# Softmax scaling and duplicate key rows moved from VectorE to ScalarE in a two-layer hybrid trunk

## The chip, the cores and the metric

The kernel runs on one core of a Trainium2 chip. A core has TensorE (matrix products, PE in the profile, with its weight loads as PEld), VectorE (DVE), ScalarE (ACT), GpSimd (POOL) and SyncE (SP), which here issues the transfers from HBM. Each engine carries out its own instructions in order and waits on semaphores for the results of the others. The metric is the device time of one execution in microseconds (us), lower is better.

## The reference

The reference is a trunk of two layers over 512 latent tokens `x` and 256 context tokens `y`, model width 1024. In each layer a normalised, modulated input is projected by `w_in`; three branches run on the parts of the projection; their gated outputs are merged and projected back.

```python
def hybrid_layer(x, y, ...):
    rq, rk, rv, rg, nq, nk, nv, ng, gq, gk, gv, gg, mg = split_cols(hx @ w_in)      # latent
    crq, ..., cgv, cgg, cmg = split_cols(hy @ w_in)                                   # context
    o_lat, o_ctx = bidir_retention(...)                    # 4 heads of 128
    na_x = neighbourhood_attention(nq, nk, nv, kc, vc, rpb, rows) * silu(ng)  # 8 heads of 64
    gqa_x = gqa_blocks(q_g, k_all, v_all) * silu(gg)        # 8 query heads, 2 key/value heads of 64
    x = x + gate_x * merge_branches(ret_x, na_x, gqa_x, mg, w_ret_o, w_na_o, w_gqa_o, w_out)
    if need_ctx:  # layer 0 only
        y = y + gate_y * merge_branches(ret_y, na_y, gqa_y, cmg, ...)

def attend(q, k, v):                      # grouped-query attention; the context's attention too
    s = einsum('btkgd,bskd->bkgts', q, k) * dh ** -0.5
    return einsum('bkgts,bskd->btkgd', softmax(s), v)

# neighbourhood attention: a query sees a window of 8 rows x 16 columns of the grid, and the context
s = where(col_ok, einsum(q, k_window) * scale + bias, -inf)
p = softmax(concatenate([s, einsum(q, k_ctx) * scale]))
```

The result is `rms_norm(x, final_norm_w)`. What matters here are the two softmaxes, neighbourhood attention (NA below) and grouped-query attention (GQA), and the keys of NA.

## The kernel before

Every product is made in split precision. A value is kept as a rounded high part and a low part (the rest), and `mm3` (L285 to L288) makes one product of three matmuls: high by high, high by low, low by high. So each operand has to be split before TensorE can use it: a ScalarE copy writes the high part, a subtraction writes the low part. For the streamed weights that is `whi` on ScalarE (L270) and `wlo` on GpSimd (L272).

The order of TensorE's instructions is written out by hand; the other engines are ordered by a scheduler that follows the order in which the code issues them, with priorities in a few places. In the code, `window()` takes two lists: the steps of a branch (scores, transposes, products with the values) and `Unit`s (projections and merges, which are long rows of matmuls on streamed weights). After each step it lets units run until their share of the work is done, so that between two dependent steps of a softmax there is independent TensorE work. The windows of the two softmax branches are `na.steps(p)` and `gqa.steps(p)`, with p from 0 to 3 in each of two layers. In the profiled execution NA of layer 0 lies at about 50 to 260 us, GQA of layer 0 at 290 to 525, NA of layer 1 at 1010 to 1160, GQA of layer 1 at 1160 to 1380. PSUM banks are few: `pj` 2, `s` 2, `pt` 3, `pv` 1.

The path of one block of probabilities, in NA's `s_step` and in GQA's:

1. TensorE makes the scores in an `s` bank (L603 in NA; L859, L860 in GQA).
2. VectorE takes them to SBUF and finds the row maximum (L606 with the bias added; L861), then makes its negative, `nm` (L613; L866, L868).
3. ScalarE takes the exponential of two tiles with `nm` as the bias and the row sum as accumulated output (L615, 128x512; L870, 128x768).
4. VectorE makes the reciprocals `rc` of both sums in one instruction (L617; L872).
5. The two tiles are scaled by `rc`: the one on VectorE, the other on GpSimd (L620; L875).
6. TensorE transposes 128x128 pieces into a `pt` bank (L632; L883).
7. `split_pt` splits the bank: ScalarE copies the high part `ph` (L446), VectorE subtracts for the low part `pl` (L447).
8. TensorE multiplies the values with `ph`, then with `pl` (L643, L644; L895).

In layer 0 each NA head has a small softmax over the context besides, `ctx_steps`: two exponentials on ScalarE (`pc`, L465), reciprocals on VectorE (`rcc`, L467), two scalings on GpSimd (L469), transposes (L477), the split, the products (L485).

The keys of NA come from the projection unit `u_k(p)`, one pair of heads at a time, in two column blocks (512 and 256). From the PSUM bank `ps`, `split_rows` (L432 to L436) writes the high parts of 64 rows on ScalarE (L434) and the low parts on VectorE (L435), for each of the two heads. The score matmul takes 128 rows: the high keys twice, one above the other. So the 64 high rows are written a second time into the other 64 partitions of the same tile, by L544 and L545.

Of the kernel before, what the change touches and what calls it, by code (L numbers as in the profile page):

```python
# [12 lines left out]
AF = mybir.ActivationFunctionType  # L13
ALU = mybir.AluOpType
# [25 lines left out]
def trunk_kernel(ctx: ExitStack, tc: tile.TileContext, xt, wcol, wv, adaw, wbr, wout, nabias, vecs,  # L40
                 cst, cst16, out, taps=None):
    nc = tc.nc
# [19 lines left out]
    def f(ap):  # L62
        return ap.bitcast(F32)
# [368 lines left out]
    def split_rows(hi, lo, rl, r0, src, scale, cols):  # L432
        rows = slice(r0, r0 + 64)
        nc.scalar.activation(hi[rows, cols], src[rows], AF.Copy, scale=scale)  # L434
        nc.vector.scalar_tensor_tensor(lo[rl:rl + 64, cols], src[rows], scale, f(hi[rows, cols]),  # L435
                                       op0=ALU.mult, op1=ALU.subtract)  # L436
# [58 lines left out]
    def pv_(P, j):  # L495
        t, pad = P[j]
        return t[:, :, pad:pad + 256]


    class NA:  # L500
# [34 lines left out]
        def u_k(self, p):  # L535
            def ev(ps, o, n):
                if o == 0:
                    self.K1[p] = [self.ap.tile([128, NT], F32R, tag="k1", name="k1", bufs=4) for _ in range(2)]
                    self.K2[p] = self.kz[p % 2]
                c = slice(o, o + n)  # L540
                K1, K2 = self.K1[p], self.K2[p]
                split_rows(K1[0], K2[0], 0, 0, ps, 1.0, c)
                split_rows(K1[1], K2[1], 64, 64, ps, 1.0, c)
                nc.vector.tensor_copy(K1[0][64:128, c], f(K1[0][0:64, c]))  # L544
                nc.vector.tensor_copy(K1[1][0:64, c], f(K1[1][64:128, c]))  # L545
            return u_proj(ap_wcol[self.l][CT_NK + p], G_ALL, ev)

        def u_v(self, p):
# [26 lines left out]
        def heads(self, p):  # L575

            ap, l = self.wp, self.l
            heads = []
            for e in range(2):
                r0 = 64 * e  # L580
                st = {}

                def start(e=e, st=st):
                    bias = ap.tile([128, 4, 256], F32, tag="bias", name="bias", bufs=2)
                    nc.sync.dma_start(out=bias[:, 0:3, :], in_=nabias[l, 2 * p + e].rearrange("p (v c) -> p v c", c=256))
                    nc.gpsimd.memset(bias[:, 3, :], 0.0)
                    pa = ap.tile([128, 2, 2, 256], F32, tag="pa", name="pa", bufs=2)
                    pb = ap.tile([128, 2, 2, 320], F32, tag="pb", name="pb", bufs=2)
                    nc.gpsimd.memset(pb[:, :, :, 0:64], 0.0)
                    P = [(pa[:, 0], 0), (pb[:, 0], 64), (pb[:, 1], 64), (pa[:, 1], 0)]  # L590
                    st.update(bias=bias, P=P)
                    for nm in ("mx", "nm", "sm", "rc"):
                        st[nm] = ap.tile([128, 4], F32, tag=nm, name=nm, bufs=2)

                def s_step(j, e=e, st=st, start=start):
                    Q, K1, K2 = self.Q[p], self.K1[p], self.K2[p]
                    if j == 0:
                        start()
                    P, bias = st["P"], st["bias"]
                    s = bank("s")  # L600
                    qc = slice(128 * j, 128 * j + 128)
                    kc = 64 * BAND0[j]
                    mm(s, lhsT=Q[e][:, qc], rhs=two_blocks(K1[e], kc, NX, 256), start=True, stop=False)  # L603
                    mm(s, lhsT=Q[e][:, qc], rhs=two_blocks(K2[e], kc, NX, 256), start=False, stop=True)
                    v = BVAR[j]
                    nc.vector.tensor_tensor_reduce(  # L606
                        out=pv_(P, j), in0=s.rearrange("p (a c) -> p a c", a=2),
                        in1=bias[:, v:4:3 - v, :], scale=1.0, scalar=-3.0e38, op0=ALU.add, op1=ALU.max,
                        accum_out=st["mx"][:, j:j + 1])
                    if j % 2 == 0:  # L610
                        return
                    h = slice(j - 1, j + 1)
                    nc.vector.tensor_scalar(st["nm"][:, h], st["mx"][:, h], -1.0, None, op0=ALU.mult)  # L613
                    for i in (j - 1, j):
                        nc.scalar.activation(pv_(P, i), pv_(P, i), AF.Exp,  # L615
                                             bias=st["nm"][:, i:i + 1], accum_out=st["sm"][:, i:i + 1])
                    nc.vector.reciprocal(st["rc"][:, h], st["sm"][:, h])  # L617
                    for i in (j - 1, j):
                        eng = nc.gpsimd if i % 2 else nc.vector
                        eng.tensor_scalar(pv_(P, i), pv_(P, i), st["rc"][:, i:i + 1], 1.0, op0=ALU.mult, op1=ALU.mult)  # L620

                jobs = [(4 + c, 0, [(j, (256, 384, 384, 256)[j] + 128 * c) for j in range(4)]) for c in range(2)]
                for t in (0, 1, 2, 3):
                    js = [j for j in range(4) if abs(j - t) <= 1]
                    jobs.append((t, js[0], [(j, 64 * (2 * t - BAND0[j]) + (0, 64, 64, 0)[j]) for j in js]))

                def t_step(i, st=st, jobs=jobs):
                    tb, q0, parts = jobs[i]
                    pt = bank("pt")
                    for a, (j, c) in enumerate(parts):  # L630
                        pj = st["P"][j][0].rearrange("p a c -> p (a c)")
                        nc.tensor.transpose(pt[:, a * 128:a * 128 + 128], pj[:, c:c + 128], ident)  # L632
                    st[i] = split_pt(pt, 128 * len(parts), ap, 3)

                def pv_step(i, e=e, st=st, jobs=jobs, r0=r0):
                    tb, q0, parts = jobs[i]
                    n = 128 * len(parts)
                    if i == 0:
                        st["ops"] = bank("pv")
                    ph, pl = st[i]  # L640
                    V = self.V[p]
                    o = st["ops"][:, 128 * q0:128 * q0 + n]
                    mm(o, lhsT=V[:, tb, e, :], rhs=ph[:, :n], start=(i == 0), stop=False)  # L643
                    mm(o, lhsT=V[:, tb, e, :], rhs=pl[:, :n], start=False, stop=(i == len(jobs) - 1))  # L644
                    if i == len(jobs) - 1:
                        pv_out(st["ops"], NX, self.get_ot(p), r0, 0)

                def smm(s, e=e):
                    Q, K1, K2 = self.Q[p], self.K1[p], self.K2[p]
                    for i in range(2):  # L650
                        qc = slice(NX + 128 * i, NX + 128 * i + 128)
                        o = s[:, 256 * i:256 * i + 256]
                        mm(o, lhsT=Q[e][:, qc], rhs=K1[e][:, NX:NT], start=True, stop=False)
                        mm(o, lhsT=Q[e][:, qc], rhs=K2[e][:, NX:NT], start=False, stop=True)
                S = [(0.7, 0.45, lambda j=j, s_step=s_step: s_step(j)) for j in range(4)]
                T = [(1.0, 0.4, lambda i=i, t_step=t_step: t_step(i)) for i in range(6)]
                PV = [(1.0, 0.4, lambda i=i, pv_step=pv_step: pv_step(i)) for i in range(6)]
                X = [] if l else list(ctx_steps(st, smm, lambda: None, lambda e=e: [self.V[p][:, 4 + c, e, :] for c in range(2)],
                                                lambda: self.get_ot(p), r0, ap, 3))
                heads.append((S, T, PV, X))  # L660
            return heads
# [28 lines left out]
    class GQA:  # L690
# [145 lines left out]
        def steps(self, p):  # L836
            ap, l = self.ap, self.l
            kv = p // 2
            Q, K1, K2, V = self.Q, self.K1[kv], self.K2[kv], self.V
# [3 lines left out]
            for e in range(2):  # L843
                for hf in range(2):
                    st = {}

                    def s_step(i, e=e, hf=hf, st=st):
                        jj, u = divmod(i, 2)
                        if i == 0:
                            st["P"] = ap.tile([128, 2, NT], F32, tag="p", name="p", bufs=2)  # L850
                            st["mx"] = ap.tile([128, 4], F32, tag="mx", name="mx", bufs=2)
                            for nm in ("nm", "sm", "rc"):
                                st[nm] = ap.tile([128, 2], F32, tag=nm, name=nm, bufs=2)
                        P, mx, nm, sm, rc = (st[x] for x in ("P", "mx", "nm", "sm", "rc"))
                        j = 2 * hf + jj
# [6 lines left out]
                                                op1=ALU.max, accum_out=mx[:, i:i + 1])  # L862
# [6 lines left out]
                        for a in range(2):  # L869
                            nc.scalar.activation(P[:, a], P[:, a], AF.Exp, bias=nm[:, a:a + 1],  # L870
                                                 scale=rqe[:, 2 * hf + a:2 * hf + a + 1], accum_out=sm[:, a:a + 1])
                        nc.vector.reciprocal(rc, sm)  # L872
                        for a in range(2):
                            eng = nc.gpsimd if a else nc.vector
                            eng.tensor_scalar(P[:, a], P[:, a], rc[:, a:a + 1], 1.0, op0=ALU.mult, op1=ALU.mult)  # L875

                    def t_step(t2, st=st):
                        pt = bank("pt")
# [614 lines left out]
```

## Time and profile before

| | |
|---|---|
| median of 3 runs | 1732.67 us (1730.77 to 1734.23) |
| the profiled execution | 1732.19 us |
| its span in the trace | 1730.4 us |
| mean granted TensorE clock | 0.993 |
| busy: PE / VectorE / ScalarE / GpSimd | 96% / 61% / 46% / 32% of the span |
| instructions of PE / VectorE / ScalarE / GpSimd | 9940 / 2201 / 1570 / 486 |

The span is the time from the first to the last instruction of the trace; the execution's own time is 1.8 us longer. A busy share is the union of an engine's instructions over the span, so an engine that is 96% busy is without work for some 70 us. In a timeline row stand the start, the duration, engine, line and operation, the tiles written and read, the shape, and in brackets the idle time before the instruction with what ended it. In a group of instructions stand the total busy time and the mean duration of one in ns. The bracketed idle time is the engine's, whatever it had been waiting for before.

### The profile page before, as it was taken

How to read it: one execution, taken by the hardware profiler on the slowest of the kernel's cores; microseconds unless marked ns; L12 is line 12 of the kernel's file. 1: busy time of each engine (PE TensorE's matmuls, PEld its weight loads, DVE VectorE, ACT ScalarE, POOL GpSimd, SP SyncE). 2: the span in 40 equal slices, each digit the busy share in tenths (PEclk: the TensorE clock that was granted, in tenths of full speed). 3: DMA queues.
4: the chain of work that ended last, by engine and by line, in shares of the span. 5: the costliest groups of instructions: out<-in, count | busy, mean ns of one | idle time of the engine just before them, and what ended most of it. 6: DMA issues, size and time to landing. Idle time of an engine off the chain costs nothing. (4 is left out here: it accounts for less than half of the span.)

```text
span 1730.4 us, 26113 instructions
## 1 busy us (share of the span) xinstructions
PE 1660.4 (96%) x9940; PEld 1438.0 (83%) x9940; DVE 1058.3 (61%) x2201; ACT 797.0 (46%) x1570; POOL 555.5 (32%) x486
## 2 busy tenths in 40 slices
PE   5999999999999999999999999999999999999996
PEld 4878888888899889888887889877787898888786
DVE  6666567666655665565324766668777646556456
ACT  4455564555553443443223445654555534444342
POOL 1423332332332222322222343433333333243432
PEclk9999999999999999999999999999999999999998
DMA  8211111111111111214536521311111222222344
GB/s 319 86 46 56 58 46 53 37 49 37 37 50 59 50 58 40 62 49 155 211 134 207 171 94 51 99 51 62 49 49 51 71 63 72 61 78 69 104 139 148
DMA packets 43053, 146.38 MB, mean 85 GB/s; under 512 B 4912, under 2 KB 10160, under 8 KB 39856
## 3 DMA queue, kind: packets, MB, share of 16 engines
q1 hardware_dynamic: 42928, 144.72, 25.2%
q8 instruction: 78, 1.28, 0.3%
q14 instruction: 47, 0.39, 0.1%
HBM read 140.51 MB, written 4.19 MB: 84 GB/s over the span
## 5 line engine op out<-in xcount | busy, mean ns | idle before, releaser
L272 POOL TENSOR_TENSOR wlo<-raw,whi 128x512 fp32r<-128x512 f32 x345 | 456.3, 1328 | 959.3 <-ACT whi L270 904.8
L286 PE MATMUL pj<-hxh,whi 128*128 128x512 f32 (+1 forms) x1192 | 429.4, 360 | 1.2 <-DVE mt L1114 1.0
L287 PE MATMUL pj<-hxl,whi 128*128 128x512 f32 (+1 forms) x1192 | 414.3, 348 | 0.0
L288 PE MATMUL pj<-hxh,wlo 128*128 128x512 f32 (+1 forms) x1192 | 414.2, 348 | 0.0
L270 ACT CAST whi<-raw 128x512 fp32r<-128x512 f32 x376 | 231.1, 618 | 282.1 <-PE pj L287 169.9
L288 PEld LDWEIGHTS pj<-hxh,wlo 128*128 128x128 f32 x1192 | 225.3, 189 | 30.4
L286 PEld LDWEIGHTS pj<-hxh,whi 128*128 128x128 f32 x1192 | 225.7, 189 | 20.3 <-DVE mt L1114 1.4
L287 PEld LDWEIGHTS pj<-hxl,whi 128*128 128x128 f32 x1192 | 226.2, 190 | 18.3
L447 DVE TENSOR_TENSOR pl<-pt,ph 128x512 fp32r<-128x512 f32 (+2 forms) x208 | 126.8, 626 | 53.9 <-ACT ph L446 51.9
L446 ACT CAST ph<-pt 128x512 fp32r<-128x512 f32 (+2 forms) x208 | 107.6, 533 | 70.5 <-PE pt L632 30.6
L286 PE MATMUL pj<-gat,whi 128*128 128x512 f32 (+1 forms) x320 | 112.2, 351 | 2.0 <-ACT gat L925 2.0
L287 PE MATMUL pj<-gat,whi 128*128 128x512 f32 (+1 forms) x320 | 110.2, 344 | 0.2 <-DVE gat L926 0.2
L288 PE MATMUL pj<-gat,wlo 128*128 128x512 f32 (+1 forms) x320 | 110.1, 344 | 0.0
L286 PE MATMUL pt<-hxh,whi 128*128 128x512 f32 (+1 forms) x256 | 96.3, 376 | 1.0 <-ACT hxh L411 1.0
L287 PE MATMUL pt<-hxl,whi 128*128 128x512 f32 (+1 forms) x256 | 95.1, 372 | 1.9 <-DVE hxl L412 1.9
L288 PE MATMUL pt<-hxh,wlo 128*128 128x512 f32 (+1 forms) x256 | 94.7, 370 | 0.0
L870 ACT ACTIVATE p<-p,nm,rq 128x768 f32<-128x768 f32 x64 | 65.4, 1024 | 46.7 <-DVE nm L868 46.1
L861 DVE TENSOR_SCALAR_CACHE_REDUCE p<-s 128x384 f32<-128x384 f32 x128 | 69.1, 555 | 27.0 <-PE s L860 25.6
L318 PE MATMUL pj<-whi,hxh 128*128 128x256 f32 x240 | 69.4, 289 | 0.0
L286 PEld LDWEIGHTS pj<-gat,whi 128*128 128x128 f32 x320 | 61.1, 191 | 9.2 <-ACT gat L925 2.5
L319 PE MATMUL pj<-wlo,hxh 128*128 128x256 f32 x240 | 68.5, 285 | 0.0
L320 PE MATMUL pj<-whi,hxl 128*128 128x256 f32 x240 | 68.5, 285 | 0.0
(304 smaller groups left out, 3529.8 us busy)
## 6 DMA issues: line engine op xcount, KB each, us to landing
raw<-in_wcol_dram SPq DMA_DIRECT2D x116, 512.0 KB, 3.5
araw<-in_adaw_dram SPq DMA_DIRECT2D x24, 1024.0 KB, 6.4
raw<-in_wout_dram SPq DMA_DIRECT2D x32, 512.0 KB, 3.5
raw<-in_wbr_dram SPq DMA_DIRECT2D x24, 512.0 KB, 3.5
raw<-in_wv_dram SPq DMA_DIRECT2D x16, 512.0 KB, 3.5
bias<-in_nabias_dram SPq DMA_DIRECT2D x16, 384.0 KB, 3.1
x<-in_xt_dram SPq DMA_DIRECT2D x8, 384.0 KB, 5.8
xo<-in_xt_dram SPq DMA_DIRECT2D x8, 256.0 KB, 3.6
```

Source lines behind the costliest of these rows:

```text
L270: nc.scalar.copy(hi, raw[:, c])
L272: lo_eng.tensor_tensor(lo, raw[:, c], f(hi), op=ALU.subtract)
L286: mm(ps, lhsT=sh, rhs=mh, start=start, stop=False)
L287: mm(ps, lhsT=sh, rhs=ml, start=False, stop=False)
L288: mm(ps, lhsT=sl, rhs=mh, start=False, stop=stop)
L318: mm(o, lhsT=sh[:, tok], rhs=hi, start=(k == 0), stop=False)
L319: mm(o, lhsT=sh[:, tok], rhs=lo, start=False, stop=False)
L320: mm(o, lhsT=sl[:, tok], rhs=hi, start=False, stop=(k == KT - 1))
L446: nc.scalar.copy(ph[:, :n], pt[:, :n])
L447: nc.vector.tensor_tensor(pl[:, :n], pt[:, :n], f(ph[:, :n]), op=ALU.subtract)
L861: nc.vector.tensor_scalar(P[:, jj, kk], s[:, :384], 1.0, -3.0e38, op0=ALU.mult, op1=ALU.max, accum_out=mx[:, i:i + 1])
L870: nc.scalar.activation(P[:, a], P[:, a], AF.Exp, bias=nm[:, a:a + 1], scale=rqe[:, 2 * hf + a:2 * hf + a + 1], accum_out=sm[:, a:a + 1])
```

## The change

Two things move. The duplicates of the high key rows were VectorE copies from the SBUF tile; they are ScalarE copies from the PSUM bank, from which the first 64 rows come. And of the two scalings of a softmax pair, the one on VectorE becomes a ScalarE instruction (a copy with `rc` as its scale); the one on GpSimd stays. The context's softmax is not changed.

```diff
@@ u_k
                 split_rows(K1[0], K2[0], 0, 0, ps, 1.0, c)
                 split_rows(K1[1], K2[1], 64, 64, ps, 1.0, c)
-                nc.vector.tensor_copy(K1[0][64:128, c], f(K1[0][0:64, c]))
-                nc.vector.tensor_copy(K1[1][0:64, c], f(K1[1][64:128, c]))
+                nc.scalar.copy(K1[0][64:128, c], ps[0:64])
+                nc.scalar.copy(K1[1][0:64, c], ps[64:128])
@@ NA, s_step
                     nc.vector.reciprocal(st["rc"][:, h], st["sm"][:, h])
-                    for i in (j - 1, j):
-                        eng = nc.gpsimd if i % 2 else nc.vector
-                        eng.tensor_scalar(pv_(P, i), pv_(P, i), st["rc"][:, i:i + 1], 1.0, op0=ALU.mult, op1=ALU.mult)
+                    nc.scalar.activation(pv_(P, j - 1), pv_(P, j - 1), AF.Copy, scale=st["rc"][:, j - 1:j])
+                    nc.gpsimd.tensor_scalar(pv_(P, j), pv_(P, j), st["rc"][:, j:j + 1], 1.0, op0=ALU.mult, op1=ALU.mult)
@@ GQA, s_step
                         nc.vector.reciprocal(rc, sm)
-                        for a in range(2):
-                            eng = nc.gpsimd if a else nc.vector
-                            eng.tensor_scalar(P[:, a], P[:, a], rc[:, a:a + 1], 1.0, op0=ALU.mult, op1=ALU.mult)
+                        nc.scalar.activation(P[:, 0], P[:, 0], AF.Copy, scale=rc[:, 0:1])
+                        nc.gpsimd.tensor_scalar(P[:, 1], P[:, 1], rc[:, 1:2], 1.0, op0=ALU.mult, op1=ALU.mult)
```

VectorE has 96 instructions less (64 scalings, 32 duplicates) and ScalarE 96 more. TensorE's order and that of the transfers are the same. Three places show how ScalarE's and VectorE's orders change.

ScalarE in GQA of layer 1, p = 0, the first two pairs of tiles (about 1209 to 1219 us of the trace of before). `p` is the tile of probabilities, `sg` a gate, `whi` a weight's high part; before:

```order
L870 ACTIVATE p,sm<-p,nm,rq 128x768 x2
L270 CAST whi<-raw 128x512
L419 ACTIVATE sg<-pj 128x512
L446 CAST ph<-pt 128x512
L870 ACTIVATE p,sm<-p,nm,rq 128x768 x2
L270 CAST whi<-raw 128x512
L446 CAST ph<-pt 128x512 x2
```

The same stretch after the change, where the exponential has line 869 and the scaling line 872:

```order
L869 ACTIVATE p,sm<-p,nm,rq 128x768 x2
L270 CAST whi<-raw 128x512
L872 ACTIVATE p<-p,rc 128x768
L419 ACTIVATE sg<-pj 128x512
L869 ACTIVATE p,sm<-p,nm,rq 128x768 x2
L270 CAST whi<-raw 128x512
L872 ACTIVATE p<-p,rc 128x768
L446 CAST ph<-pt 128x512 x3
```

Each scaling stands one weight behind its exponentials. The first `ph`, which stood ahead of the second pair of exponentials, stands behind them and behind the second scaling.

ScalarE in NA of layer 0, p = 3, the second head's last probabilities and the context's (about 231 to 235 us); `pa` and `pb` are NA's tiles, `pc` the context's; before:

```order
L615 ACTIVATE pa,sm<-pa,nm 128x512
L615 ACTIVATE pb,sm<-pb,nm 128x2x256
L446 CAST ph<-pt 128x512
L615 ACTIVATE pb,sm<-pb,nm 128x2x256
L615 ACTIVATE pa,sm<-pa,nm 128x512
L465 ACTIVATE pc,smc<-s,nmc 128x256 x2
L446 CAST ph<-pt 128x384
```

And after:

```order
L615 ACTIVATE pa,sm<-pa,nm 128x512
L615 ACTIVATE pb,sm<-pb,nm 128x2x256
L446 CAST ph<-pt 128x512
L615 ACTIVATE pb,sm<-pb,nm 128x2x256
L618 ACTIVATE pa<-pa,rc 128x512
L615 ACTIVATE pa,sm<-pa,nm 128x512
L465 ACTIVATE pc,smc<-s,nmc 128x256
L618 ACTIVATE pb<-pb,rc 128x2x256
L465 ACTIVATE pc,smc<-s,nmc 128x256
L446 CAST ph<-pt 128x384
```

Both scalings of the head (L618) now stand ahead of the second exponential of the context.

VectorE in NA of layer 0, p = 1, where the keys of the next pair are made (about 144 to 149 us); `kz` is the low part of the keys, `k` the high part, `nmc` the context's negative maximum; before:

```order
L435 SCALAR_TENSOR_TENSOR kz_566<-pj,k_1537 64x512
L544 CAST k_1537<-k_1537 64x512
L447 TENSOR_TENSOR pl<-pt,ph 128x256
L435 SCALAR_TENSOR_TENSOR kz_567<-pj,k_1538 64x512
L545 CAST k_1538<-k_1538 64x512
L460 TENSOR_REDUCE nmc<-s 128x2
L447 TENSOR_TENSOR pl<-pt,ph 128x512
```

And after:

```order
L435 SCALAR_TENSOR_TENSOR kz_566<-pj,k_1537 64x512
L447 TENSOR_TENSOR pl<-pt,ph 128x256
L460 TENSOR_REDUCE nmc<-s 128x2
L435 SCALAR_TENSOR_TENSOR kz_567<-pj,k_1538 64x512
L447 TENSOR_TENSOR pl<-pt,ph 128x512
```

The two copies that stood between the low parts of the probabilities are gone from VectorE.

## Rows read from the trace of the kernel before

**Rows 1.** The page: busy time, share of the span and instructions of each engine.
```profile
PE 1660.4 (96%) x9940; PEld 1438.0 (83%) x9940; DVE 1058.3 (61%) x2201; ACT 797.0 (46%) x1570; POOL 555.5 (32%) x486
```
**Rows 2.** TensorE's waits by releaser: us in total, times, longest.
```profile
PE pv L644 <- DVE pl L447: 6.6, 11, 1.0
PE pv L895 <- DVE pl L447: 4.5, 11, 0.8
PE s L859 <- DVE p L861: 2.7, 3, 2.1
...
PE s L603 <- DVE k L544: 2.3, 4, 1.1
...
PE pv L643 <- ACT ph L446: 1.2, 3, 0.7
```
**Rows 3.** Groups on VectorE: what moves (busy us, mean ns | idle before).
```profile
L875 DVE TENSOR_SCALAR p<-p,rc 128x768 f32<-128x768 f32 x32 | 21.4, 668 | 0.8
L544 DVE CAST k<-k 64x512 fp32r<-64x512 f32 (+1 forms) x16 | 11.5, 720 | 0.5
L620 DVE TENSOR_SCALAR pa<-pa,rc 128x512 f32<-128x512 f32 x16 | 8.6, 541 | 0.4
L620 DVE TENSOR_SCALAR pb<-pb,rc 128x512 f32<-128x512 f32 x16 | 8.4, 522 | 0.5
L545 DVE CAST k<-k 64x512 fp32r<-64x512 f32 (+1 forms) x16 | 7.2, 452 | 0.3
```
**Rows 4.** Groups on ScalarE by shape: the nearest to what is added.
```profile
L270 ACT CAST whi<-raw 128x512 fp32r<-128x512 f32 x376 | 231.1, 618 | 282.1 <-PE pj L287 169.9 <-PE pt L287 39.4 <-DMA raw<-in_wout_dram 17.0
L870 ACT ACTIVATE p<-p,nm,rq 128x768 f32<-128x768 f32 x64 | 65.4, 1024 | 46.7 <-DVE nm L868 46.1 <-DVE rc L872 0.5
L615 ACT ACTIVATE pa<-pa,nm 128x512 f32<-128x512 f32 x32 | 22.9, 717 | 14.6 <-DVE nm L613 14.5
L434 ACT ACTIVATE k<-pj 64x512 fp32r<-64x512 f32 x12 | 7.1, 593 | 7.7 <-PE pj L288 4.9 <-DVE kz L435 2.8
L925 ACT CAST gat<-ot 128x768 fp32r<-128x768 f32 x8 | 6.7, 834 | 6.2 <-DVE ot L830 3.7 <-DVE ot L1079 2.1 <-PE pj L287 0.4
L434 ACT ACTIVATE k<-pj 64x256 fp32r<-64x256 f32 x16 | 6.0, 378 | 7.3 <-DVE kz L435 7.2
```
**Rows 5.** Timeline of GQA, layer 1, p = 0, from 1211.5 to 1217.8.
```profile
1212.36 0.59 ACT L419 ACTIVATE sg<-pj 128x512 f32<-128x512 f32 x1
...
1214.26 0.47 DVE L868 TENSOR_TENSOR nm<-nm,rq 128x2 f32<-128x2 f32 x1
1214.32 0.59 ACT L446 CAST ph<-pt 128x512 fp32r<-128x512 f32 x1 [1.37 <-PE pt L883]
1214.80 1.03 ACT L870 ACTIVATE p<-p,nm,rq 128x768 f32<-128x768 f32 x1
...
1217.44 0.40 PE L895 MATMUL pv<-ph,gv 128*128 128x256 f32 x2
```
**Rows 6.** Timeline of GQA, layer 0, from 330.2 to 332.2.
```profile
330.72 0.58 ACT L446 CAST ph<-pt 128x512 fp32r<-128x512 f32 x1
...
331.35 0.50 PE L895 MATMUL pv<-ph,gv 128*128 128x256 f32 x2
```
**Rows 7.** Timeline of NA, layer 0, p = 3, from 232.3 to 236.2.
```profile
234.27 0.46 ACT L465 ACTIVATE pc<-s,nmc 128x256 f32<-128x256 f32 x1
...
235.72 0.79 PE L477 MATMUL pt<-ident,pc 128*128 128x128 f32 x2 [0.77 <-POOL pc L469]
```
**Rows 8.** Timeline of NA, layer 0, p = 1, from 145.2 to 149.2.
```profile
146.85 0.42 DVE L545 CAST k<-k 64x512 fp32r<-64x512 f32 x1
...
148.77 0.50 PE L644 MATMUL pv<-pl,v 128*128 128x512 f32 x1 [1.03 <-DVE pl L447]
```
**Rows 9.** Timeline of NA, layer 0, p = 0, from 102.5 to 104.6.
```profile
102.78 1.28 POOL L272 TENSOR_TENSOR wlo<-raw,whi 128x512 fp32r<-128x512 f32 x1 [6.10 <-ACT whi L270]
102.97 1.37 DVE L545 CAST k<-k 64x512 fp32r<-64x512 f32 x1
```

## The prediction

> **What bounds the kernel now.** I read the page's busy times first: TensorE is at work for 1660.4 of 1730.4 us, VectorE for 61% and ScalarE for 46% [rows 1]. So no engine other than TensorE bounds the kernel by its amount of work; what the change is worth is the difference that it makes to TensorE's 70 us without work. Second, the table of TensorE's waits: in the softmax stages it waits for VectorE in four ways, 6.6, 4.5, 2.7 and 2.3 us, together 16.1 us [rows 2]. The first two are for the low parts `pl`, the last for the duplicate key rows. Third, the groups on VectorE, for what goes, and those on ScalarE, for what comes. Last, the timeline at the 64 pairs of tiles, where I compared the moment at which each `ph`, `pl` and `pc` is ready with the moment at which TensorE wants it. That slack, and not the busy share, decides: ScalarE is idle for half the time, but it works in order, and a new instruction ahead of a `ph` that is wanted at once delays TensorE by its whole length.
>
> **What goes and what comes.** VectorE loses 21.4 us of GQA scaling, 8.6 + 8.4 of NA scaling and 11.5 + 7.2 of key copies, 57 us in all [rows 3]. ScalarE gains 32 scalings of 128x768, 32 of 128x512, 16 key copies of 64x512 and 16 of 64x256. The key copies have near relatives, the copies of the same rows from the same bank: 593 and 378 ns [rows 4], so 16 x 0.593 + 16 x 0.378 = 15.5 us. A ScalarE instruction that takes its scale from a tile and writes SBUF to SBUF is not in these groups. From below it is bounded by the plain copy, 834 ns at 128x768 and 618 at 128x512, from above by the exponential, 1024 and 717, which has pointer operands and the accumulation besides [rows 4]. I take the upper ends, since the scale is a pointer operand too: 32 x 1.02 + 32 x 0.72 = 56 us, of which some 0.1 us each overlaps the next instruction, so that a scaling holds ScalarE for 0.93 or 0.62 us. With the lower ends it is 0.74 or 0.52, and the terms below shrink by a fifth. ScalarE goes from 46% to about 50%, no bound.
>
> The row shows that VectorE does the 128x768 scaling in 668 ns, where ScalarE needs 834 to 1024 for the like. The Trainium skill, *ScalarE: Activation LUTs*, section "Rules for kernel authors", speaks against the change in the same sense: multiplications belong on VectorE, and it budgets about 0.3 us and 0.83 ns per element for an ACTIVATE with a pointer operand; the estimate from it is 0.94 us at 768 and 0.73 at 512, within my bounds. By it the sum below would be less than a microsecond lower.
>
> **Terms of the sum, in stalls of TensorE.**
>
> (a) GQA, layer 1, first block. Before, `ph` runs at 1214.32, ahead of the second pair of exponentials, and TensorE reads it at 1217.44 [rows 5]. The new order puts it behind both exponentials, the weight and the second scaling. The first scaling stands ahead of the gate copy of 1212.36 and moves it by 0.93; the maximum that ends at 1214.26 + 0.47 has VectorE's gate multiplication in front of it, with room for about half of that, so the exponentials start 0.45 later, near 1215.25. Two of them (1.03 each), the weight (0.62, of which 0.1 overlaps), the scaling (0.93) and the copy (0.59) end near 1219.3, which is 1.9 after TensorE wants it. `pl` takes 0.7 more, of which two matmuls hide 0.2: **+2.4**.
>
> (b) Other GQA blocks where a scaling comes just before a `ph`. The pattern: `ph` runs at 330.72 and TensorE, already waiting, reads it at 331.35 [rows 6]; the scaling in front costs its whole 0.93 and a little wait for `rc`. There are three such places (331, 1286 and 1328 us), 1.0 to 1.1 each, and four (434, 1318, 1353, 1372) where some half a microsecond of slack leaves 0.4 each: **+4.7**. At the other GQA pairs the `ph` has 1 to 5 us of slack, and units run meanwhile: nothing. Without that cover each would be 0.9.
>
> (c) NA's heads: a scaling between the exponentials and the next `ph`. Near 88 both scalings of a pair of steps count, less what slack there is, +1.5; at 1158 +1.2; at 1044 +0.6; at 1126 +0.4: **+3.7**.
>
> (d) The context's softmax in layer 0. Its second exponential ends at 234.73, and TensorE has waited 0.77 us for the scaled `pc` when it begins at 235.72 [rows 7]. Two NA scalings now stand ahead of that exponential (2 x 0.62, and 0.2 for the reciprocal): +1.4. At three other heads (120, 139 and 198 us) one scaling does, 0.7 with its reciprocal: **+3.6**. GpSimd's scalings, L469, come behind and cannot catch up.
>
> (e) Relief of VectorE. The key copies stood ahead of `pl`: one at 146.85 for 0.42, and a TensorE wait of 1.03 for `pl` ends at 148.77 [rows 8]. Without them about 1.0 goes at 106, at 149 and at 208. At the last two most of it (0.9 each) comes back at the next head's first scores, which now wait for ScalarE's duplicate, late behind its exponentials. In GQA, `pl` comes earlier where a VectorE scaling stood ahead of it: 0.6 at 392, 1.7 in 1228 to 1233, 0.4 at 1239 and 0.35 at 1273. With 0.2 at 1117: −3.0 + 1.8 − 3.05 − 0.2 = **−4.4**. In layer 1 the key copies come out even, the earlier `pl` against a PSUM bank that is held longer by two readers; the cost is covered by the matmuls of the units.
>
> 2.4 + 4.7 + 3.7 + 3.6 − 4.4 = +10.0. A stall of TensorE gives the other engines time, so that a stall behind it shrinks; I take off 1. Of the profiled execution's 1732.19 us (0.5 under the median shown) that makes 1732.19 + 9 = **1741 us**. With the lower ends for the scaling, (a) to (d) shrink from 14.4 to 11.5, and it is +6; with no taking off, +10; with places that I misjudged by their slack, +4 to +14.
>
> **Rivals.** *No change.* The scheduler and the slack take everything: ScalarE is idle 54% of the time, the two gains and losses of a few us are near each other, and the stalls that (a) to (d) foresee are each around 1 us. For it: most GQA blocks of layer 0 have slack. Against it: rows 5 and 7, where there is none. Time 1733, between 1729 and 1736.
>
> *Faster, by VectorE's relief.* Mechanism: at the VectorE scalings and key copies, `pl` or the scores come earlier, and ScalarE's additions fall into its idle time. Place: the 11 + 11 waits for `pl` [rows 2]; price: with (a) to (d) at nothing, −4.4, so 1728; at most all 16.1 us, so 1716. It decides from the point at which the `ph` behind a scaling has a microsecond of slack. A duplicate on VectorE took 1.37 us beside a GpSimd subtraction that ran from 102.78 to 104.06 [rows 9], where it takes 0.42 without one [rows 8]. That is what the Trainium skill, *SBUF — State Buffer*, section "Terms", says of the port pair that VectorE and GpSimd share: one holds it for its whole instruction and the other is blocked. By that rule the scalings and copies that leave VectorE would free GpSimd's weights too, and the change would gain more than their own time; the trace agrees at that place, but the waits of TensorE that decide are for VectorE [rows 2], so little of GpSimd's gain would reach the end.
>
> *Much slower.* ScalarE, in order, stops at each scaling until VectorE's reciprocal is there, and all that is behind, `whi` first, starts late. 64 scalings hold it for 32 x 0.93 + 32 x 0.62 = 50 us; if 40% is uncovered, +20: 1752. Against it: in GQA a weight copy stands between exponentials and scaling in most places, and in that time the reciprocal is made.
>
> **How the numbers follow.** Forecast (+4 to +14) 0.52; no change 0.20; faster 0.14; much slower 0.14. A difference under 0.2% (3.5 us) cannot be told from no change here. So faster has the 0.14 of its rival, within 0.2% the 0.20 of no change, and slower the 0.66 of the forecast and much slower together. The likeliest case alone reaches from 1736 to 1746; the range for 8 in 10 goes down to 1728, the price of the faster rival, and up to 1750, most of the way to the slower, which leaves out about half of each of these two.
>
> **What would show it.** In the trace of after: the scaling at 0.94 to 1.02 and 0.65 to 0.72 us per instruction; in the waits of TensorE a larger sum for `ph` (now 1.2 us in NA [rows 2], where I expect over 3 in NA and GQA together) and for `pc`, and a smaller one for `pl`; the first block of GQA in layer 1 with `ph` behind the second scaling and over 2 us of waiting; scores waiting for ScalarE's duplicate instead of VectorE's. I am wrong if the waits for `ph` stay under 3 us, if those for `pl` fall by more than 5, or if the scaling is much faster than a plain copy.

## The result, and the profile after

The changed kernel takes 1752.44 us in the median of 4 runs (1752.04 to 1754.88), the kernel before 1732.18 us in 4 runs on the same chip: +20.3 us, ratio 1.0116, 95% interval 1.0104 to 1.0128. The forecast was 1741, its range ended at 1750. The sign was right, the size less than half of what came. The profiled execution of the changed kernel took 1754.88 us, with a span of 1753.1 us against 1730.4.

The busy times, in answer to [rows 1]:

```profile
PE 1670.4 (95%) x9940; PEld 1445.1 (82%) x9940; DVE 1006.8 (57%) x2105; ACT 855.2 (49%) x1666; POOL 536.8 (31%) x486
```

VectorE lost 52 us of 57 reckoned. ScalarE gained 58, where 71 were reckoned: its new groups take 68 us in all, part of it overlapped with its other work. TensorE, with the same 9940 instructions, is busy 10 us longer. That it needs longer for the same work is a first sign of a lower clock.

TensorE's waits, in answer to [rows 2] (us in total, times, longest):

```profile
PE s L603 <- ACT k L544: 7.8, 6, 1.9
PE pv L893 <- ACT ph L446: 4.5, 6, 1.1
PE pv L642 <- ACT ph L446: 3.8, 3, 3.1
PE pt L477 <- POOL pc L469: 3.0, 2, 2.0
...
PE pv L893 <- DVE pl L447: 2.8, 9, 0.6
...
PE pv L643 <- DVE pl L447: 2.4, 7, 0.5
PE pt L881 <- ACT p L872: 2.2, 3, 1.5
...
PE pj L286 <- ACT k L545: 1.7, 3, 0.8
```

The waits for `pl` fell from 11.1 to 5.2 us. That they fall was expected, but by more than 5 us was one of the prediction's own signs of being wrong, and it came: by 5.9. It did not make the kernel faster, because other waits grew by more. The one for duplicate keys, 2.3 us on VectorE, became 7.8 on ScalarE, and the projections wait 1.7 for the bank that `L545` reads. The waits for `ph` rose from 1.7 to 8.3. What was added costs per instruction, in answer to [rows 4] (groups on ScalarE by shape; total, mean ns | idle before):

```profile
L872 ACT ACTIVATE p<-p,rc 128x768 f32<-128x768 f32 x32 | 29.9, 934 | 1.1 <-DVE rc L871 1.1
L618 ACT ACTIVATE pb<-pb,rc 128x512 f32<-128x512 f32 x16 | 11.6, 723 | 0.2 <-DVE rc L617 0.2
L618 ACT ACTIVATE pa<-pa,rc 128x512 f32<-128x512 f32 x16 | 11.5, 722 | 2.0 <-DVE rc L617 2.0
```

The idle time before the scalings, 3.3 us in all, is what ScalarE waited for reciprocals.

Below, a *step* is a place where TensorE loses or gains time: its instructions of two traces are matched one to one (the order is the same), and the step is the change in the distance of two neighbours. I count those of at least 0.3 us.

Of the version below with both scalings and `ph` and `pl` at high priority, the profiled one of seven executions took 3302.72 us; it is in no ratio, and that version's trace is from a further run.

### The profile page after: what moved, and what is told of

The parts are those of the page before. It is cut to its first block, busy times and chain, and to the rows that moved or that the text cites. A ratio compares the mean times of both kernels' runs of the same rounds, so it can differ in the third digit from the quotient of the medians.

```text
span 1753.1 us, 26042 instructions
## 1 busy us (share of the span) xinstructions
PE 1670.4 (95%) x9940; PEld 1445.1 (82%) x9940; DVE 1006.8 (57%) x2105; ACT 855.2 (49%) x1666; POOL 536.8 (31%) x486
```

## The experiments

All were timed beside the kernel before, whose medians were 1733.57 to 1734.78 us. A ratio is to that kernel.

| on ScalarE | median us | ratio, 95% interval |
|---|---|---|
| keys only | 1737.55 | 1.0022 (1.0012 to 1.0032) |
| NA scaling only | 1739.65 | 1.0028 (1.0017 to 1.0038) |
| GQA scaling only | 1737.20 | 1.0017 (1.0009 to 1.0026) |
| both scalings | 1748.54 | 1.0078 (1.0062 to 1.0094) |
| keys only, from SBUF | **1724.77** | 0.9944 (0.9931 to 0.9957) |
| whole change, keys from SBUF | 1739.65 | 1.0036 (1.0022 to 1.0049) |
| keys only, from PSUM, high parts first | 1733.50 | 1.0001 (0.9992 to 1.0009) |
| keys from SBUF, high parts first | 1729.49 | 0.9976 (0.9967 to 0.9985) |
| keys from SBUF; both tiles scaled on GpSimd | 1731.16 | 0.9984 (0.9975 to 0.9993) |
| both scalings, `ph` and `pl` at high priority | 1739.34 | 1.0034 (1.0021 to 1.0047) |
| keys from SBUF, `ph` and `pl` at high priority | 1727.75 | 0.9970 (0.9958 to 0.9983) |
| both scalings, extra matmuls, one group misplaced | 1744.57 | 1.0068 (1.0055 to 1.0082) |
| both scalings, extra matmuls in two waits | 1742.46 | 1.0050 (1.0036 to 1.0064) |
| whole change, extra matmuls in two waits | 1746.90 | 1.0076 (1.0059 to 1.0093) |

### Each part alone

The edits are the three parts of the diff, one at a time; then the two scalings together.

> Only the duplicate key rows on ScalarE; all scalings as before. Theory A (each part costs on its own: in the changed kernel's trace the first scores of a head wait 1.5 us each for the late duplicate at four heads and the projection 0.4 to 1.0 us for its PSUM bank at three, against 3.2 us of relief at the low parts): +4 to +7 us. Theory B (the parts cost only together, because ScalarE is filled): under +2. The prediction's own terms: -1.4 (relief 3.2, given back 1.8).

> Only the even NA tiles scaled on ScalarE. Theory A: +5 to +9 us, from ph and the context's pc behind scalings (86, 120, 236, 1153 us of the trace of before). Theory B: under +2. The prediction's terms (c) and (d): +7.

> Only the first GQA tile of a pair scaled on ScalarE. Theory A: +5 to +9 us, spread over both layers, about 3 of it in layer 0, where the scaling stands behind the next pair's first exponential and the transposes wait for it. Theory B: under +2. The prediction's terms (a), (b) and the GQA part of (e): +4.

By medians the parts cost 3.6, 5.7 and 3.3 us. Theory A gave the right signs; NA lies in its range, the other two lie under it. Theory B's bound of 2 us failed for each. The prediction's terms stand for NA (7.3 against 5.7) and, by medians, for GQA (4.0 against 3.3), and fail for the keys (-1.4 against +3.6). The sum of the parts is 12.6, 7.7 less than the whole.

> Both scalings (NA and GQA) on ScalarE, the keys as before. Alone they cost 5.7 (NA) and 3.3 us (GQA) by medians. Theory 1 (the parts add up, the excess of 8 us of the whole change over its parts comes with the keys): +8 to +10 us, 1742 to 1744. Theory 2 (the excess is general: more stalls, and a lower granted clock after them): +12 to +16 us, and a mean granted clock under 0.992.

+14.8 us: theory 2. Each step of the two runs with one scaling stands in this run at the same place with the same size to 0.05 us, but for those near 27, 561 and 1702 us, outside the softmax stages. So there is no new wait between them. Yet together they cost 5.8 us more than their sum. With the keys' 3.6 this makes 18.4, near the whole.

### The keys: what a copy from PSUM waits for

```diff
-                nc.scalar.copy(K1[0][64:128, c], ps[0:64])
-                nc.scalar.copy(K1[1][0:64, c], ps[64:128])
+                nc.scalar.copy(K1[0][64:128, c], f(K1[0][0:64, c]))
+                nc.scalar.copy(K1[1][0:64, c], f(K1[1][64:128, c]))
```

> Only the duplicate key rows on ScalarE, but copied from the SBUF tile as before, so that the PSUM bank is free as early as before. If the bank that is held longer is what costs: 2 us or more under the run with copies from PSUM. If the cost is the duplicate's place behind other work on ScalarE: within 1 us of that run, and the scores wait as long.

> The whole change, but with the duplicate key rows copied by ScalarE from the SBUF tile and not from PSUM. Theory 1 (the copies from PSUM are what costs with the keys; all else adds up): -9.2 + 5.7 + 3.3 = about 0, 1732 to 1736. Theory 2 (ScalarE filled by the three parts together costs whatever the source): 1738 or more.

The same copies on the same engine, from the other source, are 12.8 us faster: 9 us under the kernel before, where the copies from PSUM were 3.6 above it. In the whole change the source is worth 12.8 too (1752.4 to 1739.65, against a kernel before that was 1.6 slower in that session). The first expectation named two causes, the bank that is held longer and a late place on ScalarE; the bank (2 us) was the smaller, and the late place came from the source. In the second the time fits theory 2, but not its reason: the scalings add 14.9 us to the keys copied from SBUF and 14.8 to the keys on VectorE, so they cost the same whether or not ScalarE has the keys. The timeline at the first scores of layer 1, copies from PSUM:

```profile
1031.74 0.38 ACT L434 ACTIVATE k<-pj 64x256 fp32r<-64x256 f32 x1
1032.15 0.42 DVE L435 SCALAR_TENSOR_TENSOR kz<-pj,k 64x256 fp32r<-64x256 f32 x1 [1.72 <-ACT k L434]
1032.60 0.38 ACT L434 ACTIVATE k<-pj 64x256 fp32r<-64x256 f32 x1 [0.48 <-DVE kz L435]
1033.01 0.43 DVE L435 SCALAR_TENSOR_TENSOR kz<-pj,k 64x256 fp32r<-64x256 f32 x1 [0.45 <-ACT k L434]
1033.47 0.36 ACT L544 CAST k<-pj 64x256 fp32r<-64x256 f32 x1 [0.49 <-DVE kz L435]
1033.86 0.37 ACT L545 CAST k<-pj 64x256 fp32r<-64x256 f32 x1
...
1033.88 0.50 PE L603 MATMUL s<-k,q 128*128 128x512 f32 x1 [1.89 <-ACT k L544]
```

And copies from SBUF:

```profile
1025.89 0.38 ACT L434 ACTIVATE k<-pj 64x256 fp32r<-64x256 f32 x1
...
1026.30 0.41 ACT L544 CAST k<-k 64x256 fp32r<-64x256 f32 x1
1026.30 0.42 DVE L435 SCALAR_TENSOR_TENSOR kz<-pj,k 64x256 fp32r<-64x256 f32 x1 [1.00 <-ACT k L434]
...
1026.75 0.38 ACT L434 ACTIVATE k<-pj 64x256 fp32r<-64x256 f32 x1
1026.76 0.50 PE L603 MATMUL s<-k,q 128*128 128x512 f32 x1
```

The instructions that read `pj`, one PSUM bank, stand in turn: ScalarE, VectorE, ScalarE, VectorE, each idle until the other engine has done. A low part needs its high part in any case; but the second high part waits for the first low part, and the duplicate for the second, although the rows that they read differ. These waits end with semaphores of the other engine, so it is the program that keeps the order. A duplicate from PSUM joins this line at its end, 1.73 us behind the first high part (1031.74 to 1033.47). From SBUF it needs only that high part, comes 0.41 behind it (1025.89 to 1026.30), beside VectorE's reading of the bank, and no wait is left at the scores. The bracket at `DVE L435` of the second listing shows that this line of turns is there in any case.

The Trainium skill, *PSUM — Partial Sum Buffer*, section "PSUM bank collisions raise a hardware error", says that two engines must not touch the same bank in the same group of 32 partitions at once, two readers included, and that other groups of partitions are free. The trace agrees that two readers don't overlap; but it shows the turns also between rows 0 to 63 and 64 to 127, and whether the chip needs them there no run here shows.

The next two change the order of the readers:

```diff
-                split_rows(K1[0], K2[0], 0, 0, ps, 1.0, c)
-                split_rows(K1[1], K2[1], 64, 64, ps, 1.0, c)
+                split_rows(K1[0], K2[0], 0, 0, ps, 1.0, c, 0)       # 0: the high part alone
+                nc.scalar.copy(K1[0][64:128, c], ps[0:64])
+                split_rows(K1[1], K2[1], 64, 64, ps, 1.0, c, 0)
+                nc.scalar.copy(K1[1][0:64, c], ps[64:128])
+                split_rows(K1[0], K2[0], 0, 0, ps, 1.0, c, 1)       # 1: the low part alone
+                split_rows(K1[1], K2[1], 64, 64, ps, 1.0, c, 1)
```

The second of them does the same with the copies' source in SBUF, and issues the high parts of NA's queries ahead of their low parts as well.

> Only the key copies on ScalarE, from PSUM, but issued with the high parts: high 0, duplicate 0, high 1, duplicate 1 on ScalarE, then both low parts on VectorE. If what costs is that readers of one PSUM bank on two engines come one after the other (ScalarE, VectorE, ScalarE, VectorE, and the duplicates last of all), the scores' wait for the duplicate falls from 7.9 to under 3 us and the time to 1725 to 1731. If a copy from PSUM is itself what costs: 1736 to 1739 as in the first run with keys.

> Key copies on ScalarE from SBUF, and for the keys and queries of NA both high parts ahead of both low parts, so that a PSUM bank changes its reader once and not three times. By the theory of readers in turn: 1 to 4 us under the run with copies from SBUF (1724.8), the projection's waits for the bank smaller. Otherwise no change or up to +3, since the low parts come later.

From PSUM, with the duplicates among the high parts, no wait for the duplicate is among TensorE's larger ones, and 4 us come back: the duplicate's place behind the turns cost that much. The time, 1733.5, lies between the two that the expectation named, since 8.7 us remain to the copies from SBUF, at other places. Four ScalarE instructions in a row now stand ahead of `ph` (142 to 147 us of that trace):

```profile
141.88 0.59 ACT L435 ACTIVATE k<-pj 64x512 fp32r<-64x512 f32 x1 [0.33 <-PE pj L288]
142.48 0.58 ACT L545 CAST k<-pj 64x512 fp32r<-64x512 f32 x1
143.07 0.59 ACT L435 ACTIVATE k<-pj 64x512 fp32r<-64x512 f32 x1
143.68 0.58 ACT L547 CAST k<-pj 64x512 fp32r<-64x512 f32 x1
...
145.98 0.97 ACT L448 CAST ph<-pt 128x512 fp32r<-128x512 f32 x2
...
146.62 0.49 PE L647 MATMUL pv<-ph,v 128*128 128x512 f32 x1 [1.18 <-ACT ph L448]
```

Two steps of 1.34 and two of 0.40 against the copies from SBUF are such. Others are at the low key parts, which come later now (three of 0.3 to 0.4), and at the projections that wait for their bank (0.60 and 0.75). Changing the order with the source in SBUF is no gain but a loss of 4.7 us; the expectation missed that by more than its margin. With the readers in turn and the copies from SBUF, `ph` runs between the key copies (at 142.60 and 144.24 us of that trace).

### The scalings: ScalarE's order

Both tiles of a pair on GpSimd, with the keys copied from SBUF; and, with the scalings on ScalarE, the split at the priority that the weights have:

```diff
-                        eng = nc.gpsimd if i % 2 else nc.vector
+                        eng = nc.gpsimd
...
+        with tc.high_priority(PRI):
             nc.scalar.copy(ph[:, :n], pt[:, :n])
             nc.vector.tensor_tensor(pl[:, :n], pt[:, :n], f(ph[:, :n]), op=ALU.subtract)
```

> Keys copied by ScalarE from SBUF; both tiles of every pair scaled on GpSimd, so that neither VectorE nor ScalarE has the work. If the cost of the scalings is that they stand in ScalarE's order ahead of ph and the exponentials: under the run with scalings on ScalarE (1739.7), 1728 to 1736, though the transposes wait 0.9 us more for the second tile at places. If what costs is only that the pair's second tile comes late: 1738 or more.

> Both scalings on ScalarE, keys as before, and ph and pl issued at high priority, so that ph stands ahead of scalings and exponentials where both are ready. If ScalarE's order is the cost: 3 to 8 us under the run without the priority (1748.5), TensorE's waits for ph under 4 us. If it is ScalarE's added work, wherever it stands: within 2 us of it; and where exponentials now come later, more.

> A look at the trace of the run with both scalings on ScalarE and ph and pl at high priority, whose time was 1739.3 us. If ScalarE's order is the cost: TensorE's waits for ph, 7.7 us with the scalings alone, are under 3 us, and those for exponentials or scalings have not grown as much.

They bear out that the place in ScalarE's order costs. With all scalings on GpSimd the time is 8.5 us under that with scalings on ScalarE; it is still 6.4 above scalings on VectorE, because the transposes now wait 9.2 us in 10 places for a tile from GpSimd (1.2 in 3 places before). With priority for `ph` and `pl` the kernel with the two scalings is 4.6 us over the kernel before and not 14.8. It is 9.2 us under the run without the priority, where 3 to 8 were expected. How much of this is `pl`, which the priority moves too, is not shown. The trace of the further run, of 1741.05 us, has no wait for `ph` among its 22 largest. It has new ones of 4.4 for a query's low part and 4.0 for a head's output, and the transposes wait 6.4 us for a scaling, 2.3 without the priority.

> Key copies on ScalarE from SBUF, scalings on VectorE as before, ph and pl at high priority: a candidate for the fastest. By the theory of ScalarE's order 1 to 4 us under 1724.8, since some waits for ph and pl (8 us in that run) go; the risk is later exponentials, up to +3.

A miss: 3 us slower. Without scalings on ScalarE, `ph` ahead of all delays other things: TensorE waits 3.3 us for reciprocal norms, 3.3 for a head's output and 2.5 for a query that it didn't wait for. Against that, all but 1.0 of the 7.8 us of waits for `pl` went. By the estimate of the section on the clock, what turns this into a loss is the granted clock: its median is 0.9905, against 0.994 without the priority.

### The clock

> Both scalings on ScalarE, keys as before, and in two waits of TensorE (first head of layer 0 before its first product with the values, 3 us; last head of layer 0 before the context's transposes, 2 us) 11 and 8 extra matmuls that write a bank which is overwritten afterwards. If the excess of the two scalings over their sum (5.8 us) is the lower granted clock that follows waits: the stretches at half clock near 88 and 238 us are gone, the mean clock rises by 0.001 to 0.002, and the time is 1.5 to 3.5 us under the run without the extra matmuls (1748.5). If the clock has no part in it: the same or up to 1 us more.

> Both scalings on ScalarE, keys as before, with the extra matmuls in the first head's wait (11) and now in front of the transposes of the context's softmax of the first head of the last pair, where the wait of 2 us at 238 us is (8; the earlier run had them at the second head's, where nothing waits). If the lower clock after a wait is part of the cost: no stretch at half clock near 88 or 238 us, 1741 to 1744.5. If not: 1747 or more.

> The whole change with the same extra matmuls. If the clock is part of the cost: 3 to 7 us under the changed kernel (1752.4), mean clock at least 0.992, no stretch at half clock near 90 and 240 us. If not: 1751 to 1754.

```diff
+                def fill(ps, n, e=e):
+                    for x in range(n):
+                        mm(ps, lhsT=self.Q[p][e][:, 0:128], rhs=self.K1[p][e][:, 0:512], start=True, stop=True)
...
+                        if (l, p, e) == (0, 0, 0):
+                            fill(st["ops"], 11)
```

The first of the three had its second group where nothing waited, and paid 1.8 us for it; still the time fell. With both groups in waits, 19 matmuls that do nothing useful take 6.1 us from the two scalings and 5.5 from the whole change. The stretch from 88 to 96 us by windows (busy us of PE, PEld, DVE, ACT and POOL with counts, granted clock, DMA share, GB/s), in the kernel before:

```profile
88.00:96.00 8.00, 7.82 (x35) 6.62 (x36) 4.23 (x9) 3.35 (x9) 1.84 (x3) 0.79 0.11 44
```

With both scalings on ScalarE:

```profile
88.00:96.00 8.00, 6.52 (x29) 5.42 (x30) 4.35 (x8) 3.77 (x9) 1.28 (x1) 0.79 0.15 58
...
238.00:246.00 8.00, 6.97 (x36) 5.97 (x37) 5.34 (x11) 4.40 (x12) 0.93 (x2) 0.79 0.01 2
```

In the changed kernel, the 4 us ahead of it too, then the waits at both places:

```profile
84.00:88.00 4.00, 1.80 (x16) 1.60 (x14) 1.22 (x3) 3.98 (x10) 2.67 (x3) 1.00 0.38 106
88.00:96.00 8.00, 7.08 (x24) 5.73 (x25) 3.94 (x8) 3.04 (x7) 1.28 (x1) 0.57 0.13 54
...
240.00:248.00 8.00, 7.65 (x42) 6.73 (x42) 5.04 (x10) 4.39 (x11) 0.25 (x2) 0.79 0.01 2
...
88.88 0.80 PE L642 MATMUL pv<-ph,v 128*128 128x512 f32 x1 [3.08 <-ACT ph L446]
...
239.81 1.00 PE L477 MATMUL pt<-ident,pc 128*128 128x128 f32 x4 [2.00 <-POOL pc L469]
```

And in the whole change with the extra matmuls:

```profile
84.00:88.00 4.00, 4.00 (x28) 3.64 (x27) 1.05 (x4) 3.98 (x11) 2.70 (x3) 1.00 0.38 105
88.00:96.00 8.00, 7.08 (x38) 5.60 (x37) 4.54 (x9) 4.78 (x12) 1.37 (x2) 1.00 0.15 60
...
240.00:248.00 8.00, 7.61 (x57) 6.85 (x56) 6.00 (x12) 5.26 (x14) 2.23 (x3) 1.00 0.00 0
```

In the changed kernel TensorE was at work for 1.8 of 4 us, then the clock fell to the lower of its two levels, 1.2 instead of 2.4 GHz: up to 8 x (1 - 0.57) = 3.4 us are lost there, and 8 x (1 - 0.79) = 1.7 from 240 to 248, behind a wait of 2.0. The first of these stretches is in the kernel before too, at 0.79, so part of what the extra matmuls gain is not the change's.

The mean clock of all runs gives the clock's share in sum: its median is 0.9905 with both scalings, 0.993 and 0.994 with one. An estimate of a kernel's time at full clock is each run's time multiplied by its own mean clock, as if all of the time followed the clock. The means of these are 1720.8 before (without one run that has an entry of 0.944 at an ordinary time), 1725.1 with the keys alone, 1726.5 NA, 1726.8 GQA, 1731.5 both scalings and 1735.9 the whole change. So the parts cost 4.3, 5.7 and 6.0, the two scalings 10.7 and the whole 15.1: no excess over the sums is left. Between runs of one kernel 0.001 of clock goes with 1.2 us, and not with the 1.7 that this takes. With 1.2 the whole costs 16.4 and its parts 15.1 together, so most of the excess is the clock's either way. With the extra matmuls the estimates are 1731.6 and 1735.7, as without them: most or all of what they gain is clock. The priority without scalings, a miss by time, is 1711.6 against 1715.0 without it.

Which wait brings which stretch is less clear. In the profiled executions, up to 20 us before the end, the lower level was granted for 13.7 us before, 17.1 in each part alone, 27.3 with both scalings, 30.7 with the whole change and 13.7 in each of the two with matmuls in both waits. But of the 13.7 us that both scalings add to the kernel before, only 3.4, at 240, stand behind one of the change's larger waits; others, near 1247 and 1622, have their like in the traces of single parts.

The Trainium skill, *TensorE: Matmul & The Clock Gate*, section "HAM oscillation — how this bites in real kernels", describes a kernel that pays for waits twice: for the wait, and for a stretch at the lower clock that begins its next work. This trace agrees at 88 and 240 us, behind waits of 3.1 and 2.0 us.

## Why the prediction was wrong, point by point

**The step that failed is the key copies in (e),** put at -1.4 us and measured at +3.6 alone. Their relief was right: 1.0 each was forecast at three places, and the steps are 1.03, 1.10 and 1.11 with the keys alone. What was to be given back was put at 1.8 in layer 0 and at nothing in sum in layer 1. Measured were steps of 0.64, 1.46 and 1.47 in layer 0 and, in layer 1, 1.57 at the first scores and 0.42, 0.97 and 0.57 at projections that wait for their bank: 7.1 in all, against 3.2 of relief. The prediction took the duplicate to be late because of exponentials ahead of it, and the bank to be covered. It had not seen that the rows of before already show the turns: L434 there has an idle time that ends with L435 [rows 4], and a copy from PSUM that is issued last stands behind them all. The relief in GQA, put at 3.05, held: the steps are 0.94 at 392, 0.95 in 1228 to 1233, 0.77 at 1241 and 0.36 at 1274.

**The clock was not a term.** The prediction took 1 us off, because other engines catch up during a wait. No such gain shows: the steps of the parts come back unshrunk with both scalings. And the granted clock fell, with 5.8 us between the two scalings and their sum. By the estimate of the section on the clock most of this or all is the clock's, and of the whole change's 20 us some 15 to 16 are waits and 4 to 5 the clock. Where each stretch at the lower clock comes from stays open in part, since one profile shows the stretches of one execution.

**(a)** forecast 2.4; the steps are 1.17 and 0.38, so 1.5. The order was as foreseen:

```profile
1234.90 0.93 ACT L872 ACTIVATE p<-p,rc 128x768 f32<-128x768 f32 x1
1235.74 1.52 ACT L446 CAST ph<-pt 128x512 fp32r<-128x512 f32 x3
...
1236.35 0.51 PE L893 MATMUL pv<-ph,gv 128*128 128x256 f32 x2 [1.01 <-ACT ph L446]
```

The delay by the first scaling, 0.45, did not come about: the maximum was no later. So the wait is 1.01 and not over 2.

**(b)** held: at the three places without slack ([rows 6] is the first) the steps are 0.82 each, for 1.0 to 1.1. Of four places at 0.4 one came (0.49). Instead others came that I had not listed. At 359 us of the trace of before (+1.3) the scaling stands behind the next pair's first exponential, and the transposes wait for it:

```profile
364.91 0.15 DVE L871 RECIPROCAL rc<-sm 128x2 f32<-128x2 f32 x1
...
365.08 1.03 ACT L869 ACTIVATE p<-p,nm,rq 128x768 f32<-128x768 f32 x1 [0.46 <-DVE rc L871]
...
366.11 0.92 ACT L872 ACTIVATE p<-p,rc 128x768 f32<-128x768 f32 x1
...
367.08 0.66 PE L881 MATMUL pt<-ident,p 128*128 128x128 f32 x4 [1.54 <-ACT p L872]
```

The reciprocal was there at 365.06, but the scaling began at 366.11, behind the exponential, and the transposes at 367.08. At 447 (+0.9) transposes wait 0.8 us behind VectorE's sum of squares, and not for a scaling; at 1242 `ph` and `pl` come 0.9 later; at 318 and 420 there are 0.4 each. Gains were missed too: 0.6 at 360 and 0.5 each at 1305 and 1350, where transposes had waited for GpSimd's tile. In sum GQA alone cost 3.3 by medians for a forecast 4.0; but its runs had higher clocks than the kernel before, and with the clock taken out it is 5 to 6, so that the agreement of the medians is partly luck.

**(c) and (d)** held in sum, 7.3 for a measured 5.7: 1.7 at 88 (forecast 1.5), 1.0 at 1158 (1.2), 0.7 at 1126 (0.4), 1.2 at 236 (1.4) and 0.6 at 120 (0.7). At 1044 0.5 came for 0.6, at 139 0.3 for 0.7, at 198 a gain of 0.3 for a loss of 0.7, and 1.5 at 1153, where scores wait for a VectorE maximum, was not listed.

**The durations** were right: 934 ns at 128x768 between bounds of 834 and 1024, and 722 at 128x512, just above 717.

**The rivals.** "Much slower" named 1752, which came, but that is luck: its mechanism did not come, since ScalarE waited only 3.3 us for reciprocals before its scalings. "Faster" described the wrong edit: relief alone would have needed the duplicates somewhere where they hardly wait, and the copies from SBUF are that, at -9 us. GpSimd did become faster, as that rival had it: its scalings of 128x768 take 919 ns for 1258. Of that TensorE got the gains of 1.6 us named under (b) and 0.4 at 1117.

## What to carry to other kernels

When a copy is moved to another engine, ask first what its source is and who else reads that: the duplicate read from SBUF gained 9 us, the same read from PSUM lost 4. An engine that is idle half of the time is not free if it works in order; a 0.9 us instruction ahead of one that is wanted at once costs nearly its whole length. And small waits of the bounding engine are not the whole cost: look at its granted clock behind them, and set each run's mean clock beside its time before you compare parts with a whole, since 0.001 of it goes here with 1.2 us or more.

## What the runs showed of the hardware that was not expected

ScalarE and VectorE never read the `pj` bank of the keys at the same time in the listings above, though a copy from SBUF runs fully beside such a read (1026.30 on both engines). And 19 useless matmuls made a kernel 5.5 us faster, because a TensorE that works through its waits kept the granted clock at 1.00 where it had been at 0.57 and 0.79. How often a stretch at half clock comes differs between executions: those of both scalings had mean clocks of 0.990 to 0.993 and times from 1749.3 to 1743.1 us, the lowest time at the highest clock.
